# Running sums kept in device memory, and products that start on filled banks, in a hybrid attention block

## The chip, the core and the metric

The kernel runs on one core of a Trainium2 chip. The metric is the device time of one execution in microseconds; smaller is better. A core has five engines with a queue of instructions each: TensorE (PE; its weight loads are shown as PEld), VectorE (DVE), ScalarE (ACT), GpSimd (POOL) and SyncE (SP). Each runs its instructions in the order of the program and waits on semaphores where it needs another's result. Transfers are issued from SP's queue, and, where they add to what is at their destination, from GpSimd's.

## The reference, cut to what matters

The program is one decoder block on 512 tokens of width 2048, in float32. The attention half (two head groups, of 8 heads each) is not touched by the change, apart from one small step. What matters here is the second half:

```
h = h + mixed @ w_out                       # h: 512 x 2048, the residual
hn2 = rmsnorm(h, norm2_g)
h = h + (silu(hn2 @ w_gate) * (hn2 @ w_up)) @ w_down      # hidden width 5632
return rmsnorm(h, final_g)
```

## The kernel before, in words

All matrices lie transposed: 128 features on the partitions, 512 tokens along the free axis. Every weight tile is split into a high part (fp32r, ScalarE, L136) and the rest (VectorE, L139), and each product is the sum of three matmuls: high by high, high by low, low by high. The tile of a split is called a half: 128x512 of weights, four 128x128 matrices. `next_half` (L174) hands out halves in the order of the list `jobs`; before it does, `split_to` issues the splits three halves ahead (`first` is the optional preparation on VectorE and the high part on ScalarE, `second` the low part and what follows it, such as the load of a later tile). Five buffers hold the split halves, so a split waits for TensorE to be done with the half five before. `later(n, f)` puts a step f into the program when n more halves have been handed out; this is how the evacuations of a product are placed between the splits on VectorE's and ScalarE's queues.

The feed-forward part has 44 blocks of 128 hidden features (`FB`). For a block, gate and up are computed together by Strassen's scheme in Winograd's form: seven products P1 to P7 instead of eight, each of two halves, each half 4 x 3 matmuls of 128 x 128 by 128 x 256 tokens. The operands on the token side (B11, T1 and so on) are made once. The weight combinations are made block by block on VectorE in place in the raw tiles (`comb`, L778). The order in a block is P1, P7, P4, P6, P5, P2, P3 (`ORDER`). P2 is added onto P1's bank and P3 onto P5's by TensorE itself; all other sums of products are made by VectorE from the banks (`after`, L1055 to L1089), in the two tiles g and u. Then come Silu on ScalarE (L1045), u*g on VectorE (L1048), its high part h on ScalarE (L1049) and its low part on VectorE (L1053). These last steps of a block run while the next block's first products are on TensorE.

After every four blocks, in the block with f%4 == 0, 16 down products (`down`, L1091) are put between that block's products, 24 matmuls each, and VectorE adds each one's bank to the residual `hs` (L1106), which lies in SBUF as 16 tiles of 128x512. In the first round it also multiplies `hs` by `inv` (L1105), which undoes the norm's scaling. The last four blocks' down products are in `last` (L1132), which also does the final norm and the output.

Each raw weight tile (128x1024) is loaded on SP's queue into one of four buffers (`LA`), at the places named in `quad_jobs` (`nxt`). Tiles made by `placed` begin 16 or 32 elements into their buffer. The token-side operands begin at 32, the split weights of the feed-forward part at 16, except for the halves marked `even`: the first half of P1 in blocks 1 and 2 and where f%8 == 5 (L819).

Of the kernel before, what the change touches and what calls it, by code (L numbers as in the profile page):

```python
# [71 lines left out]
def block_kernel(ctx: ExitStack, tc: tile.TileContext, xt, wst, wdn, smalls, wg, w2c, bias, ident_in, out):  # L72
# [5 lines left out]
    base = ctx.enter_context(tc.tile_pool(name="base", bufs=1))  # L78
    wp = ctx.enter_context(tc.tile_pool(name="wp", bufs=1))
    ps = ctx.enter_context(tc.tile_pool(name="ps", bufs=1, space=bass.MemoryType.PSUM))  # L80

    def placed(pool, n, at, **kw):

# [315 lines left out]
    def compressed(s):  # L399
        pt = ps.tile([128, 512], F32, tag="misc", name="phidt")  # L400
        for hb in range(2):
            for i in range(2):
                pe.matmul(pt[:, 64 * hb:64 * hb + 64], hids[:, s, 128 * hb:128 * hb + 128],
                          ident[:, 64 * i:64 * i + 64], start=(i == 0), stop=(i == 1))
        h = hidt[s]
        for hb in range(2):
            c = slice(64 * hb, 64 * hb + 64)
            if s == 0:
                act.activation(h[:, hb, 0, :], pt[:, c], AF.Silu)
            else:  # L410
                for g in range(2):
                    c = slice(64 * hb + 32 * g, 64 * hb + 32 * g + 32)
                    act.activation(h[:, hb, g, :, :], pt[:, None, c].to_broadcast([128, 3, 32]), AF.Silu)
        yield
        p2 = ps.tile([128, 512], F32, tag="misc", name="pcmp")
        if s == 0:
            for hb in range(2):
                pe.matmul(p2[:, :64], w2[:, hb, :], h[:, hb, 0, :], start=(hb == 0), stop=(hb == 1))
            dve.tensor_copy(kc, p2[:, :64])
        else:  # L420
            for g in range(2):
                for hb in range(2):
                    pe.matmul(p2[:96, 128 * g:128 * g + 128], h[:, hb, g, :, :],
                              w2[:, 2 + hb, :], start=(hb == 0), stop=(hb == 1))
                v = et_h[:, 7 + 3 * g, :]
                act.activation(v[:96], p2[:96, 128 * g:128 * g + 128], AF.Copy)
                dve.tensor_tensor(v[32:64], p2[32:64, 128 * g:128 * g + 128], v[32:64].bitcast(F32), op=OP.subtract)
# [336 lines left out]
    def load_fin(n):  # L764
        while len(fin) < min(n, KB // 2):
            k = 2 * len(fin)
            fin.append(wp.tile([128, 1024], F32, tag="raw", name="fin", bufs=LA))
            sp.dma_start(fin[-1].rearrange("p (n c) -> p n c", n=2), wdn[NPH - 1, k:k + 2].rearrange("n p c -> p n c"))

    def quad_jobs(f, order):  # L770
# [17 lines left out]
        for k in range(2):  # L788
            A11, A21, A22, A12 = (lambda i=i, k=k: q(i, k) for i in range(4))

            if f == 0:
                r["P1", k] = Job(A11, load=None if k else nxt(-1), post=fetch(A11, 1, k))
                r["P5", k] = Job(A21, post=fetch(A21, 0, k))
                r["P7", k] = Job(A11)
                r["P2", k] = Job(A12)
                r["P4", k] = Job(A22, prep=comb(A12, A21))
                r["P6", k] = Job(A21)
                r["P3", k] = Job(A12)
            else:
# [62 lines left out]
    def close_attention():  # L862
# [16 lines left out]
        def close():  # L879
# [8 lines left out]
            rest["hs"] = ffn.tile([128, KB, S], F32, name="hs")  # L888
# [61 lines left out]
    def terms(nb):  # L950
# [41 lines left out]
        def s3():  # L992
            dve.scalar_tensor_tensor(t[:, HI], k[:, LO], gk, t[:, LO], op0=OP.mult, op1=OP.add)
            low("T3", n, t[:, LO])
            high("T2", n, t[:, HI])

        def s4():
            dve.scalar_tensor_tensor(t[:, LO], h[:, LO], g, t[:, HI], op0=OP.mult, op1=OP.subtract)
            low("T2", n, t[:, HI])
            high("T4", n, t[:, LO])  # L1000

        def s5():
# [16 lines left out]
             for n, t in (("P1", "proj"), ("P7", "proj"), ("P4", "sc"), ("P6", "sc"), ("P3", "t"))}  # L1019
    banks["P5"] = ps.tile([128, 512], F32, tag="o", name="P5")  # L1020
    dbanks = {}

    st = {}

    def product(f, name):
        key = {"P2": "P1", "P3": "P5" if f else "P3"}.get(name, name)
        if key == name:
            st[key] = banks[name]
        p = st[key][:, :256]
# [1 line left out]
        for k in range(2):  # L1031
            h, l = next_half()
            for s in range(4):
                mm(p, h[:, 128 * s:128 * s + 128], l[:, 128 * s:128 * s + 128], th[:, 4 * k + s, :],
                   tl[:, 4 * k + s, :], key == name and k == 0 and s == 0, k == 1 and s == 3)

    def mm(o, wh, wl, mh, ml, start, stop):
        pe.matmul(o, wh, mh, start=start, stop=False, skip_group_check=True)  # L1038
# [16 lines left out]
    def after(f, name):  # L1055
# [10 lines left out]
        g, u = st.get("g"), st.get("u")  # L1066
        if name == "P1":
            st["g"] = ft()
            st["u"] = ft() if f else None
            act.activation(st["g"][:, LO], x("P1"), AF.Copy)  # L1070
        elif name == "P6":
            sub(g[:, HI], g[:, LO], x("P6"))
            add(u[:, LO], g[:, HI], x("P7"))
            if not f:
                dve.tensor_tensor(g[:, LO], x("P1"), st["r2"][:, LO], op=OP.mult)
                add(u[:, HI], u[:, LO], x("P5"))
                sub(u[:, LO], u[:, LO], x("P4"))
                add(g[:, HI], g[:, HI], x("P5"))
        elif name == "P5":
            add(u[:, HI], u[:, LO], x("P5"))  # L1080
            sub(u[:, LO], u[:, LO], x("P4"))
        elif name == "P2":
            dve.tensor_tensor(g[:, LO], x("P1"), st["r2"][:, LO], op=OP.mult)
            if f == FB - 1:
                finish(f, g, u, LO)
        elif name == "P3":
            add(g[:, HI], g[:, HI], x("P5" if f else "P3"))
            dve.tensor_tensor(g[:, HI], g[:, HI], st["r2"][:, HI], op=OP.mult)
            finish(f, g, u, HI if f == FB - 1 else slice(0, 512))  # L1089

    def down(ph, nb):  # L1091
# [9 lines left out]
                   al[:, 12 + i, c], i == 0, i == PH - 1)  # L1101

        def add():
            if not ph:
                dve.tensor_tensor(hs[:, nb, :], hs[:, nb, :], st["inv"], op=OP.mult)  # L1105
            dve.tensor_tensor(hs[:, nb, :], hs[:, nb, :], p, op=OP.add)  # L1106

        later(1, add)

    for kind, a, b in sched:  # L1110
        if kind == "d":
# [20 lines left out]
    def last():  # L1132
        todo = deque()
        sacc = ft("sacc")
        sqt = ft("sqt")
# [4 lines left out]
        def scaled(r, nb, n, th):  # L1140
            h = hs[:, nb:nb + n, (LO, HI)[th]]
            o = h
            if th:
                if nb % 4 == 0:
                    st["o"] = wp.tile([128, 1024], F32, tag="raw", name="scaled", bufs=LA)
# [134 lines left out]
```

## Time and profile before

| | us |
|---|---|
| median of 3 runs | 2176.18 |
| lowest, highest | 2175.72, 2179.32 |
| the profiled execution | 2175.39 |
| its span, first to last instruction | 2173.6 |

| engine | busy us | share of the span |
|---|---|---|
| PE | 2159.9 | 99% |
| PEld | 2021.9 | 93% |
| DVE | 1566.0 | 72% |
| ACT | 965.9 | 44% |
| POOL | 42.7 | 2% |

The feed-forward blocks begin at 836 us and the last stage at about 2110 us. Rows of the profile have the form: line, engine, operation, tile written <- tiles read, partitions x elements and types, count | busy us, mean ns of one | idle time before them and what ended it. Rows of the timeline begin with the start and the duration in us. Matmuls overlap, so a duration of 0.28 us is not the distance from one to the next; that distance is read from the starts. Rows of a stage have its limits, its length, and then the busy time and count of PE, PEld, DVE, ACT and POOL, the granted clock, the DMA share and GB/s; where one engine was asked for, only its own.

### The profile page before, as it was taken

The page shows a single profiled execution, that of the slowest core. Times are in us where ns is not written, and L with a number is a line of the kernel's source. Part 1 is how long each engine was busy: PE and PEld are TensorE (multiplying, and loading weights), DVE is VectorE, ACT ScalarE, POOL GpSimd, SP SyncE. Part 2 cuts the span into 40 slices and gives each one's busy share as a digit, 9 for nine tenths or more (in the row PEclk, how much of TensorE's full clock was granted, in tenths as well). Part 3 has the DMA queues.
Part 4 walks back from the last instruction along what each step waited for, and adds up shares of the span by engine and source line. Part 5 has one row for each costly group of instructions (what it writes and reads, how often), then busy time and mean ns, then how long its engine had stood idle before and what let it go on. Part 6 is the DMA issues. An engine that isn't in the chain of part 4 may idle for free.

```text
span 2173.6 us, 39728 instructions
## 1 busy us (share of the span) xinstructions
PE 2159.9 (99%) x15776; PEld 2021.9 (93%) x15776; DVE 1566.0 (72%) x3046; ACT 965.9 (44%) x1862; POOL 42.7 (2%) x51
## 2 busy tenths in 40 slices
PE   9999999999999999999999999999999999999997
PEld 7888888888888889999999999999999999999997
DVE  6755565456667588979687777869596877878686
ACT  6544444344444255525343443435253434434356
POOL 0000000000000000000000000000000000000003
PEclk9999999999999999999999999999999999999999
DMA  6442222322224334333333333333333333333233
GB/s 224 150 135 80 90 77 70 102 80 81 80 78 164 98 97 101 115 116 100 108 105 117 97 109 106 108 96 108 117 98 107 108 117 92 114 107 108 81 124 107
DMA packets 81866, 232.28 MB, mean 107 GB/s; under 512 B 8848, under 2 KB 11536, under 8 KB 81680
## 3 DMA queue, kind: packets, MB, share of 16 engines
q1 hardware_dynamic: 80960, 228.17, 33.4%
q0 software_dynamic: 720, 1.57, 0.4%
q8 instruction: 124, 2.03, 0.4%
q14 instruction: 62, 0.51, 0.1%
HBM read 225.51 MB, written 4.19 MB: 106 GB/s over the span
## 4 chain that ended last, share of the span: by engine, by line
PE 98%; DVE 1%; ACT 0%; DMA 0%; issue 0%; SPq 0%; DVEq 0%; ACTq 0%
PE P L1040 15%; PE P L1038 15%; PE P L1039 15%; PE pp L167 7%; PE pp L169 7%; PE pp L168 7%; PE pd L1040 4%; PE pd L1039 4%; PE pd L1038 4%; PE pab L169 3%; PE pab L167 3%; PE pab L168 3%; PE pt L533 1%; PE po L168 1%; PE psc L169 1%; PE po L167 1%
## 5 line engine op out<-in xcount | busy, mean ns | idle before, releaser
L136 ACT ACTIVATE wh<-raw 128x512 fp32r<-128x512 f32 x888 | 548.7, 628 | 528.0 <-PE P L1039 208.7
L139 DVE TENSOR_TENSOR wl<-raw,wh 128x512 fp32r<-128x512 f32 x888 | 599.5, 687 | 43.9 <-ACT wh L136 42.5
L1040 PE MATMUL P<-ah,wl 128*128 128x256 f32 x1552 | 428.9, 276 | 0.2 <-DVE wl L139 0.2
L1038 PE MATMUL P<-ah,wh 128*128 128x256 f32 x1552 | 428.8, 276 | 0.0
L1039 PE MATMUL P<-al,wh 128*128 128x256 f32 x1552 | 428.8, 276 | 0.0
L1040 PEld LDWEIGHTS P<-ah,wl 128*128 128x128 f32 x1552 | 291.4, 188 | 0.4 <-DVE wl L139 0.4
L1039 PEld LDWEIGHTS P<-al,wh 128*128 128x128 f32 x1552 | 291.4, 188 | 0.0
L1038 PEld LDWEIGHTS P<-ah,wh 128*128 128x128 f32 x1552 | 291.4, 188 | 0.0
L167 PE MATMUL pp<-ah,wh 128*128 128x512 f32 x640 | 260.6, 407 | 0.0
L169 PE MATMUL pp<-ah,wl 128*128 128x512 f32 x640 | 251.1, 392 | 0.0
L168 PE MATMUL pp<-al,wh 128*128 128x512 f32 x640 | 250.3, 391 | 0.0
L778 DVE TENSOR_TENSOR raw<-raw 128x512 f32<-128x512 f32 x346 | 237.7, 687 | 3.4
L1040 PE MATMUL pd<-ah,wl 128*128 128x256 f32 x784 | 216.6, 276 | 0.0
L1039 PE MATMUL pd<-al,wh 128*128 128x256 f32 x784 | 216.5, 276 | 0.0
L1038 PE MATMUL pd<-ah,wh 128*128 128x256 f32 x784 | 216.5, 276 | 0.0
L136 ACT ACTIVATE wh<-rawd 128x512 fp32r<-128x512 f32 x160 | 101.1, 632 | 249.1 <-PE pd L1039 122.9
L1106 DVE TENSOR_TENSOR hs<-hs,pd 128x512 f32<-128x512 f32 x98 | 67.4, 688 | 122.0 <-PE pd L1040 121.7
L1038 PEld LDWEIGHTS pd<-ah,wh 128*128 128x128 f32 x784 | 147.2, 188 | 0.0
L1040 PEld LDWEIGHTS pd<-ah,wl 128*128 128x128 f32 x784 | 147.2, 188 | 0.0
L1039 PEld LDWEIGHTS pd<-al,wh 128*128 128x128 f32 x784 | 147.2, 188 | 0.0
L169 PEld LDWEIGHTS pp<-ah,wl 128*128 128x128 f32 x640 | 120.2, 188 | 28.1 <-DVE wl L139 0.4
L139 DVE TENSOR_TENSOR wl<-rawd,wh 128x512 fp32r<-128x512 f32 x160 | 110.1, 688 | 42.6 <-ACT wh L136 37.5
(275 smaller groups left out, 4560.0 us busy)
## 6 DMA issues: line engine op xcount, KB each, us to landing
raw<-in_wst_dram SPq DMA_DIRECT2D x310, 512.0 KB, 3.5
rawd<-in_wdn_dram SPq DMA_DIRECT2D x160, 256.0 KB, 2.6
bias<-in_bias_dram SPq DMA_DIRECT2D x16, 320.0 KB, 3.0
xc<-in_xt_dram SPq DMA_DIRECT2D x16, 256.0 KB, 3.0
hs<-in_xt_dram SPq DMA_DIRECT2D x16, 256.0 KB, 5.4
fin<-in_wdn_dram SPq DMA_DIRECT2D x8, 512.0 KB, 4.1
out_dram<-hs SPq DMA_DIRECT2D x8, 256.0 KB, 2.1
out_dram<-scaled SPq DMA_DIRECT2D x3, 512.0 KB, 2.8
```

Of the source, the lines that this page charges most:

```text
L136: act.activation(self.h, self.src(), AF.Copy)
L139: dve.tensor_tensor(self.l, self.src(), self.h.bitcast(F32), op=OP.subtract)
L167: pe.matmul(o, wh, mh, start=start, stop=False)
L168: pe.matmul(o, wh, ml, start=False, stop=False)
L169: pe.matmul(o, wl, mh, start=False, stop=stop)
L533: pe.transpose(p[:, 128 * (o + b):128 * (o + b) + 128], self.e[t][:, 128 * b:128 * b + 128], ident)
L778: return lambda: dve.tensor_tensor(o(), o(), x(), op=OP.add)
L1038: pe.matmul(o, wh, mh, start=start, stop=False, skip_group_check=True)
L1039: pe.matmul(o, wh, ml, start=False, stop=False, skip_group_check=True)
L1040: pe.matmul(o, wl, mh, start=False, stop=stop, skip_group_check=True)
L1106: dve.tensor_tensor(hs[:, nb, :], hs[:, nb, :], p, op=OP.add)
```

## The change

- The residual goes to device memory. In blocks 1 and 2, `put_away` multiplies a tile of `hs` by `inv` and stores it in `kept_sums`; the tile's SBUF is given back. A down product's bank is copied by ScalarE to one of four staging tiles, and a transfer from GpSimd's queue adds it to `kept_sums`. In blocks 41 and 42 `bring_back` loads the 16 tiles into SBUF again.
- The order in a block becomes P1, P4, P6, P5, P7, P2, P3. ScalarE copies P1's bank onto P6's, and P6's products are added on it by TensorE; the sum is copied onto P7's bank, and P7 is added there. P3 is added onto P6's bank. ScalarE also copies P4's and P5's banks to u and g. VectorE is left with five operations on banks or on their sums in place of seven. The signs of the operand T2 and of some sums change with this.
- The weight combinations are placed after P1 and before P6 accordingly; the raw tiles get a fifth buffer (`RB`), with loads still four units ahead, and the second and third tile of the next block are loaded after P7.
- Smaller edits: the gains are loaded from ScalarE's queue, the two small products of the compressed values stand before both of their copies, four of block 0's eight spreads are made by ScalarE, and block 0's product of P1 with the norm's factors moves ahead of other sums.

```diff
+    mem = ctx.enter_context(tc.tile_pool(name="mem", bufs=1, space=bass.MemoryType.DRAM))
+    kept_sums = [mem.tile([128, S], F32, name=f"sums{nb}") for nb in range(KB)]
...
+    RB = 5
...
-            t = wp.tile([128, 1024], F32, tag="raw", name="raw", bufs=LA)
+            t = wp.tile([128, 1024], F32, tag="raw", name="raw", bufs=RB)
...
-        def __init__(self, col):
+        def __init__(self, col, on_act=False):
...
-                dve.tensor_scalar(self.r[:, 128 * t:128 * t + 128], ident, col[:, t:t + 1], None, op0=OP.mult)
+                r = self.r[:, 128 * t:128 * t + 128]
+                if on_act:
+                    act.activation(r, ident, AF.Copy, scale=col[:, t:t + 1])
+                else:
+                    dve.tensor_scalar(r, ident, col[:, t:t + 1], None, op0=OP.mult)
...
-    sp.dma_start(sm, smalls)
+    act.dma_start(sm, smalls)
...
                     pe.matmul(p2[:96, 128 * g:128 * g + 128], h[:, hb, g, :, :],
                               w2[:, 2 + hb, :], start=(hb == 0), stop=(hb == 1))
+            for g in range(2):
                 v = et_h[:, 7 + 3 * g, :]
...
-                r["P1", k] = Job(A11)
-                r["P7", k] = Job(A11, prep=comb(A11, A21))
+                r["P1", k] = Job(A11, post=comb(A11, A21))
                 r["P4", k] = Job(A22, post=comb(A21, A22))
+                r["P6", k] = Job(A22, prep=comb(A22, A11))
                 r["P5", k] = Job(A21)
-                r["P6", k] = Job(A22, prep=comb(A22, A11))
+                r["P7", k] = Job(A11)
...
-                r["P5", 1].post = nxt(1)
+                r["P7", 1].post = nxt(2)
...
-    ORDER = ("P1", "P7", "P4", "P6", "P5", "P2", "P3")
+    ORDER = ("P1", "P4", "P6", "P5", "P7", "P2", "P3")
...
-            high("T2", n, t[:, HI])
+            high("T2", n, t[:, HI], -1.0)
...
+    SEEDED = ("P6", "P7")
...
-        key = {"P2": "P1", "P3": "P5" if f else "P3"}.get(name, name)
+        key = {"P2": "P1", "P3": "P6" if f else "P3"}.get(name, name)
...
-                   tl[:, 4 * k + s, :], key == name and k == 0 and s == 0, k == 1 and s == 3)
+                   tl[:, 4 * k + s, :], not (f and name in SEEDED) and key == name and k == 0 and s == 0, k == 1 and s == 3)
...
             st["g"] = ft()
-            st["u"] = ft() if f else None
-            act.activation(st["g"][:, LO], x("P1"), AF.Copy)
+            if f:
+                st["u"] = ft()
+                st["P6"] = banks["P6"]
+                act.activation(x("P6"), x("P1"), AF.Copy)
+            else:
+                act.activation(st["g"][:, LO], x("P1"), AF.Copy)
         elif name == "P6":
-            sub(g[:, HI], g[:, LO], x("P6"))
+            if f:
+                st["P7"] = banks["P7"]
+                act.activation(x("P7"), x("P6"), AF.Copy)
+                act.activation(u[:, LO], x("P4"), AF.Copy)
+                return
+            add(g[:, HI], g[:, LO], x("P6"))
+            dve.tensor_tensor(g[:, LO], x("P1"), st["r2"][:, LO], op=OP.mult)
             add(u[:, LO], g[:, HI], x("P7"))
...
-        elif name == "P5":
-            add(u[:, HI], u[:, LO], x("P5"))
-            sub(u[:, LO], u[:, LO], x("P4"))
+        elif name == "P7":
+            act.activation(g[:, HI], x("P5"), AF.Copy)
+            sub(u[:, LO], x("P7"), u[:, LO])
+            add(u[:, HI], x("P7"), g[:, HI])
...
-            add(g[:, HI], g[:, HI], x("P5" if f else "P3"))
+            if f:
+                add(g[:, HI], x("P6"), g[:, HI])
+            else:
+                add(g[:, HI], g[:, HI], x("P3"))
...
-            if not ph:
-                dve.tensor_tensor(hs[:, nb, :], hs[:, nb, :], st["inv"], op=OP.mult)
-            dve.tensor_tensor(hs[:, nb, :], hs[:, nb, :], p, op=OP.add)
+            t = st["pool"].tile([128, S], F32, tag="stg", name="stg", bufs=4)
+            act.activation(t, p, AF.Copy)
+            pool_e.dma_start(kept_sums[nb], t, accum_op=OP.add)
...
+    def put_away(nb):
+        dve.tensor_tensor(hs[:, nb, :], hs[:, nb, :], st["inv"], op=OP.mult)
+        sp.dma_start(kept_sums[nb], hs[:, nb, :])
...
+    def bring_back(nb):
...
+        sp.dma_start(st["hs"][:, nb, :], kept_sums[nb])
...
+        if name == "P5" and f in (1, 2):
+            for n in range(8):
+                later(n, lambda nb=8 * (f - 1) + n: put_away(nb))
+        if name == "P5" and f in (FB - 3, FB - 2):
+            for n in range(8):
+                later(n, lambda nb=8 * (f - FB + 3) + n: bring_back(nb))
...
-                later(1, lambda r=r: st.update(inv=Spread(r.z), r2=Spread(r.y)))
+                later(1, lambda r=r: st.update(inv=Spread(r.z, True), r2=Spread(r.y)))
...
-        elif name in ("P1", "P6", "P5", "P2", "P3"):
+        elif name in ("P1", "P6", "P7", "P2", "P3"):
```

In the kernel after the change the lines have moved down a little: the copy onto P6's bank is L1084, u*g L1060, its high part h L1061, the staging copy L1129.

More of the change, by code (lines that the diff above doesn't have):

```diff
@@ L766, in load_fin @@
             k = 2 * len(fin)
-            fin.append(wp.tile([128, 1024], F32, tag="raw", name="fin", bufs=LA))
+            fin.append(wp.tile([128, 1024], F32, tag="raw", name="fin", bufs=RB))
             sp.dma_start(fin[-1].rearrange("p (n c) -> p n c", n=2), wdn[NPH - 1, k:k + 2].rearrange("n p c -> p n c"))
@@ L887, in close @@
                                    for x, at in (("h", MH), ("l", ML)))
-            rest["hs"] = ffn.tile([128, KB, S], F32, name="hs")
+            for _ in range(2):
+                ffn.tile([128, S], F32, tag="ft", name="ft", bufs=2)
+            rest["hsp"] = ExitStack()
+            rest["hs"] = rest["hsp"].enter_context(tc.tile_pool(name="hsp", bufs=1)).tile([128, KB, S], F32, name="hs")
             for nb in range(KB):
@@ L994, in s3 @@
             low("T3", n, t[:, LO])
-            high("T2", n, t[:, HI])
+            high("T2", n, t[:, HI], -1.0)
         def s4():
             dve.scalar_tensor_tensor(t[:, LO], h[:, LO], g, t[:, HI], op0=OP.mult, op1=OP.subtract)
-            low("T2", n, t[:, HI])
+            low("T2", n, t[:, HI], -1.0)
             high("T4", n, t[:, LO])
@@ L1068, in after @@
             st["g"] = ft()
-            st["u"] = ft() if f else None
-            act.activation(st["g"][:, LO], x("P1"), AF.Copy)
-        elif name == "P6":
-            sub(g[:, HI], g[:, LO], x("P6"))
-            add(u[:, LO], g[:, HI], x("P7"))
-            if not f:
-                dve.tensor_tensor(g[:, LO], x("P1"), st["r2"][:, LO], op=OP.mult)
-                add(u[:, HI], u[:, LO], x("P5"))
-                sub(u[:, LO], u[:, LO], x("P4"))
-                add(g[:, HI], g[:, HI], x("P5"))
-        elif name == "P5":
+            if f:
[4 more added lines that the diff above has]
+                act.activation(st["g"][:, LO], x("P1"), AF.Copy)
+        elif name == "P6":
+            if f:
[5 more added lines that the diff above has]
+            dve.tensor_tensor(g[:, LO], x("P1"), st["r2"][:, LO], op=OP.mult)
+            add(u[:, LO], g[:, HI], x("P7"))
             add(u[:, HI], u[:, LO], x("P5"))
             sub(u[:, LO], u[:, LO], x("P4"))
+            add(g[:, HI], g[:, HI], x("P5"))
+        elif name == "P7":
+            act.activation(g[:, HI], x("P5"), AF.Copy)
+            sub(u[:, LO], x("P7"), u[:, LO])
+            add(u[:, HI], x("P7"), g[:, HI])
         elif name == "P2":
@@ L1103, in add @@
         def add():
-            if not ph:
-                dve.tensor_tensor(hs[:, nb, :], hs[:, nb, :], st["inv"], op=OP.mult)
-            dve.tensor_tensor(hs[:, nb, :], hs[:, nb, :], p, op=OP.add)
+            t = st["pool"].tile([128, S], F32, tag="stg", name="stg", bufs=4)
+            act.activation(t, p, AF.Copy)
+            pool_e.dma_start(kept_sums[nb], t, accum_op=OP.add)
         later(1, add)
+    def put_away(nb):
+        dve.tensor_tensor(hs[:, nb, :], hs[:, nb, :], st["inv"], op=OP.mult)
+        sp.dma_start(kept_sums[nb], hs[:, nb, :])
+        if nb == KB - 1:
+            rest["hsp"].close()
+            st["dnp"] = ExitStack()
+            st["pool"] = st["dnp"].enter_context(tc.tile_pool(name="dnp", bufs=1))
+    def bring_back(nb):
+        if nb == 0:
+            st["dnp"].close()
+            st["hs"] = ctx.enter_context(tc.tile_pool(name="fin", bufs=1)).tile([128, KB, S], F32, name="hs")
+        sp.dma_start(st["hs"][:, nb, :], kept_sums[nb])
     for kind, a, b in sched:
@@ L1144, in scaled @@
                 if nb % 4 == 0:
-                    st["o"] = wp.tile([128, 1024], F32, tag="raw", name="scaled", bufs=LA)
+                    st["o"] = wp.tile([128, 1024], F32, tag="raw", name="scaled", bufs=RB)
                 o = st["o"].rearrange("p (a b) -> p a b", b=256)[:, nb % 4:nb % 4 + n, :]
```

1 line of the change is left out of this document (added).

## The prediction

> **What bounds the kernel now.** I read the page first, then the matmul rows one by one, then VectorE's and ScalarE's rows of one block. The page names TensorE, and one stage of the feed-forward part, asked for by itself, names it without a remainder.
>
> ```profile
> span 2173.6 us, 39728 instructions
> PE 2159.9 (99%) x15776; PEld 2021.9 (93%) x15776; DVE 1566.0 (72%) x3046; ACT 965.9 (44%) x1862; POOL 42.7 (2%) x51
> ...
> 880.90:1516.20 635.30, 635.30 (x5605) 635.30 (x5605) 504.57 (x857) 271.09 (x453) 0.00 (x0) 1.00 0.35 107
> ```
>
> From 880.9 to 1516.2 us TensorE is busy 635.30 of 635.30 us. The columns after it are weight loads, VectorE (504.57), ScalarE (271.09), GpSimd, granted clock, DMA share. Busy is not yet peak, so I look at the distance between matmul starts.
>
> ```profile
> 867.78 0.28 PE L1039 MATMUL P<-al,wh 128*128 128x256 f32 x1
> 868.25 0.39 PE L1040 MATMUL P<-ah,wl 128*128 128x256 f32 x1 [0.19 <-DVE wl L139]
> 868.47 0.28 PE L1038 MATMUL P<-ah,wh 128*128 128x256 f32 x1
> ...
> 869.53 0.28 PE L1038 MATMUL P<-ah,wh 128*128 128x256 f32 x1
> ...
> 879.42 0.28 PE L1038 MATMUL P<-B11h,wh 128*128 128x256 f32 x1
> ...
> 1497.17 0.28 PE L1038 MATMUL P<-B11h,wh 128*128 128x256 f32 x1
> ...
> 1516.21 0.28 PE L1038 MATMUL P<-B11h,wh 128*128 128x256 f32 x1
> ```
>
> A block has seven products of two halves, a half has 12 matmuls. Block 23 runs from 1497.17 to 1516.21: 168 matmuls in 19.04 us, 113.3 ns each, 1.360 us a half. From 869.53 to 879.42 lie 84 matmuls of the same form in 9.89 us: 117.7 ns each, 1.413 us a half. That second pitch began after a wait (867.78 to 868.25) and lasted until block 2's first half, which takes its weights from the other offset (`even`). So TensorE has two pitches here, and one short wait cost more afterwards than while it lasted. Only blocks 1, 2 and f%8==5 have such an `even` half. The work left on TensorE does not change, so this stage cannot gain; it can only keep its pitch or lose it.
>
> **What the change can give.** Two waits of the profile are aimed at.
>
> ```profile
> PE pcmp L423 <- DVE et_h L427: 0.7, 1, 0.7
> ...
> PE P L1038 <- DVE ft L1075: 0.3, 1, 0.3
> ```
>
> The two products of L423 now stand before both copies: 0.6 off, a copy's semaphore round trip being all that is left. In block 0 the multiplication that frees P1's bank (L1075) moves from third to second place and four of the eight spreads go to ScalarE: 0.4 off with its restart. The gains' load (L280) moves from SP's queue to ScalarE's, where it stands behind the first activation; x and weights start earlier, the gains later, and the first split needs both: 0, between +0.5 and -0.5. Together -1.0 us.
>
> **The cost, part by part.** The 160 additions of down products leave VectorE, 16 multiplications stay but move to blocks 1 and 2, and 160 ScalarE copies with 160 transfers come in:
>
> ```profile
> L1106 DVE TENSOR_TENSOR hs<-hs,pd 128x512 f32<-128x512 f32 x98 | 67.4, 688 | 122.0 <-PE pd L1040 121.7
> L1105 DVE TENSOR_TENSOR hs<-hs,prb 128x512 f32<-128x512 f32 x16 | 10.9, 680 | 0.0
> ...
> L1045 ACT ACTIVATE ft<-ft 128x512 f32<-128x512 f32 x43 | 27.3, 635 | 16.1 <-DVE ft L1088 16.1
> ...
> raw<-in_wst_dram SPq DMA_DIRECT2D x310, 512.0 KB, 3.5
> ...
> out_dram<-hs SPq DMA_DIRECT2D x8, 256.0 KB, 2.1
> ...
> raw<-in_wst_dram POOLq DMA_DIRECT2D x4, 256.0 KB, 4.2
> ```
>
> VectorE waited 122 us for the products before these additions, so taking them away frees no time on the path. A copy of 128x512 costs ScalarE about 0.635 us; it has 2.72 us (24 matmuls) per down product: hidden. The adding transfers of before take 4.2 us from issue to landing, into SBUF. A staging buffer (four) is wanted again after four down products, 10.9 us, less the copy: 10.2. No row shows a transfer that adds into device memory; I bound it by 2.1 (a plain store of 256 KB, to the output) and 8.4 (twice the adding one): hidden at both ends, so I take 0. The 16 stores of put_away (SP's queue, blocks 1 and 2) and the 16 loads back (blocks 41 and 42) stand ahead of weight loads; the stores wait for one VectorE operation each, the loads for additions that ended a block before: 0, as a weight load is issued four halves or more before its use. The tightest is A21's, issued behind P7's last low part, about 4 us before P2, and wanted 2.1 us into P2: 6 us for a landing of 3.5, also 0; the fifth raw buffer is what lets the next A11 come while the old one still serves P7. The changed signs ride on operations that were there. The Trainium skill ("DMA: Bandwidth & Descriptors", Anatomy of one DMA) puts a GpSimd transfer at 2.0 us plus bytes/436e3, 2.6 us here as an estimate, and warns that the wait for completion is long above all when the target is HBM; by either figure the sum stays as it is.
>
> What is not hidden is the new way to P6. P6's first matmul now waits until ScalarE has copied P1's result onto P6's bank. That copy (L1084) stands in ScalarE's queue behind h (L1061), which waits for VectorE's u*g (L1060). TensorE reaches P6 two halves after P1's end, since P4 alone lies between. So the question is when u*g is done. Its rows in before, block 22 into 23:
>
> ```profile
> 1491.73 0.28 PE L1038 MATMUL P<-B21h,wh 128*128 128x256 f32 x1
> ...
> 1492.08 0.41 DVE L1061 TENSOR_TENSOR ft<-ft,P 128x256 f32<-128x256 f32 x1
> 1492.53 0.42 DVE L1064 TENSOR_TENSOR ft<-ft,P 128x256 f32<-128x256 f32 x1
> 1492.87 0.68 DVE L139 TENSOR_TENSOR wl<-raw,wh 128x512 fp32r<-128x512 f32 x1
> 1493.59 0.69 DVE L778 TENSOR_TENSOR raw<-raw 128x512 f32<-128x512 f32 x1
> 1494.19 0.69 DVE L139 TENSOR_TENSOR wl<-raw,wh 128x512 fp32r<-128x512 f32 x1
> ...
> 1497.37 0.42 DVE L1061 TENSOR_TENSOR ft<-ft,P 128x256 f32<-128x256 f32 x1
> ...
> 1501.30 0.69 DVE L1048 TENSOR_TENSOR ft<-ft 128x512 f32<-128x512 f32 x1
> ...
> 1497.31 0.63 ACT L136 ACTIVATE wh<-raw 128x512 fp32r<-128x512 f32 x1 [0.73 <-PE P L1039]
> 1498.29 0.64 ACT L1045 ACTIVATE ft<-ft 128x512 f32<-128x512 f32 x1 [0.35 <-DVE ft L1088]
> 1498.82 0.61 ACT L136 ACTIVATE wh<-raw 128x512 fp32r<-128x512 f32 x1
> ...
> 1502.02 0.64 ACT L1049 ACTIVATE ah<-ft 128x512 fp32r<-128x512 f32 x1 [1.09 <-DVE ft L1048]
> 1502.56 0.36 ACT L1070 ACTIVATE ft<-P 128x256 f32<-128x256 f32 x1
> ```
>
> Start-to-start on VectorE they give 0.34 after a 128x256, 0.45 if the next needs it, 0.60 after a 128x512, 0.72 if the next touches the same tile; VectorE starts 0.20 after the product it waits for ends (1497.17, 1497.37), ScalarE 0.14 (1497.31); ScalarE's next follows a 128x512 after 0.53. Already in before, with u*g at 1501.30, a copy behind h ended at 1502.92. Now zero is the start of P2 (1491.73), and the next block's P6 is wanted eight halves later, at 10.88. VectorE's order in the changed kernel from there, with those steps: P7's first subtraction 0.20; the addition needs ScalarE's new copy of P5, which runs behind a weight split (0.14 + 0.53 + 0.36): 1.07; low part 1.41, combination 2.13, low 2.73, combination 3.45, P2's product 4.05, low 4.39, combination 4.99, P6's combination 5.71, low 6.31, combination 6.91, P3's addition 7.51 (P3 ended at 5.44), product 7.97, combination 8.31, low 8.91, low 9.70 (behind Silu and its split on ScalarE, 9.03 to 9.66), u*g 10.30 to 10.99. Then h 11.02, the copy 11.56 to 11.92, TensorE about 12.0: **late by 1.1 us**, or by 0.7 where the halves take 1.413 (wanted at 11.30). In before u*g stood at 9.57. Two combinations more stand ahead of it, and the chain starts with a wait for ScalarE. Without that wait and the same-tile steps it is late by 0.1 (in the 113 pitch); with one more step of 0.6, by 1.7. I take 1.1, since every step has a row.
>
> Block 4k+1 is free of it: the down products before it leave VectorE idle, so the chain starts at P3's end, 5.64, and needs about 4.4 to the copy's end: 10.2 at worst. P7's copy has two halves, 2.72 us, and needs 1.1: free.
>
> Block 1 in before, with the start of its third product and its u*g:
>
> ```profile
> 864.95 0.28 PE L1038 MATMUL P<-T4h,wh 128*128 128x256 f32 x1
> ...
> 866.30 0.69 DVE L1048 TENSOR_TENSOR ft<-ft 128x512 f32<-128x512 f32 x1
> ```
>
> The sum, over the blocks:
> - 29 blocks from 6 to 43 and block 4 are late. In 5 of them (6, 14, 22, 30, 38: the block before was put right by its `even` half) 1.1 each, 5.5; in 25, 0.7 each, 17.5.
> - Blocks 2 and 3 also have put_away's eight multiplications before them, four inside the chain at 0.60: 1.1 + 0.7 + 2 x 2.4 = 6.6. Block 1, whose chain starts behind block 0's six evacuations, I put 3.0 later than now (u*g at 866.30 already in before; a copy would end 1.62 later, as in the walk, and P6, now third, is wanted where the third product starts, 864.95 less block 0's 0.4: 3.4 late, of which block 1 has 0.4 now).
> - The first matmul behind a wait takes 0.11 more (868.25 to 868.47): 33 times, 3.6.
> - After each wait the pitch stays at 117.7 ns until the next `even` half: block 2's last 10 halves, 3, 4, then of every eight blocks all but the `even` one and four halves, 814 halves with the down products counted double, and some 23 in the last stage: 837 x 0.053 = 44.4.
> - Gains: -1.0.
>
> 5.5 + 17.5 + 6.6 + 3.0 + 3.6 + 44.4 - 1.0 = 79.6. The profiled execution took 2175.4 us (span 2173.6 and 1.8 around it), 0.8 under the median of 2176.2: 2175.4 + 79.6 = **2255 us**.
>
> **The rivals.**
> - *It waits, but the pitch comes back by itself* (0.10). All late blocks then cost 1.1: 33.0 + 7.0 + 3.0 + 3.6 - 1.0 = 45.6, 2221 us. Against it: the nine halves from 868.25 to 879.42 did not come back.
> - *Not slower: the copy comes in time* (0.13). If u*g comes 1.1 us sooner than walked, no block waits, the pitch holds and only the gains stay: 2174 us. It is decided at the addition behind P5's copy: were VectorE not behind by the time of P3's addition (5.64 instead of 7.51), the copy would end at 10.1. Against it: the list of steps from 1.07 has 13 large operations at 0.60, 7.8 us by itself.
> - *The transfers that add don't land in time* (0.05). Above 10.2 us a landing holds ScalarE, and each microsecond over costs one per four down products, 40 in all: at 12 us 72 more, above 2300.
> - *The waits bring the clock down* (0.04). At the start the same warm-up product runs at two rates:
>
> ```profile
> 1.43:4.21 2.78, 2.78 (x15) 1.00 0.77 200
> 4.33:5.22 0.89, 0.89 (x11) 1.00 0.98 325
> ```
>
> 15 in 2.78 us against 11 in 0.89: less than half the rate for 2.8 us. If each of the 33 waits brought that back, half of 2.8 us is lost each time, 46 us instead of the pitch's 44.4, on top of all blocks at 1.1: about 2267 us. The wait at 868 did not do so. The Trainium skill ("TensorE: Matmul & The Clock Gate", A second HAM failure mode) tells of such short idles between groups bringing the clock down; by it this rival would hold, and the matmuls after 868.47 do not agree.
>
> **How the numbers follow.** The forecast has 0.68; its own range is 2234 (late by 0.5 and 0.1) to 2270 (0.4 more). The range of 8 in 10 leaves out the not-slower case: 2205, below the second case, to 2280. The bound of 0.2% is 4.4 us, about what a measurement can tell from no change. The not-slower case falls mostly inside it: faster 0.04, same 0.09, slower 0.87.
>
> **What would show it.** TensorE's waits name ScalarE's L1084 before P6 some 33 times, about 1 us each, none in blocks 5, 9, 13; halves take 1.41 us after them and 1.36 behind block 5's first; h sits behind u*g; no wait of ScalarE's staging copy (L1129) for a transfer; TensorE at 2100 us of busy time or more. Wrong if P6 starts on time in block 6, or if its matmuls return to 113 ns within a half.

## The result, and the profile after

| | before | after |
|---|---|---|
| median, us | 2175.95 | 2262.54 |
| lowest to highest, us | 2174.80 to 2179.94 | 2250.55 to 2265.61 |
| the profiled execution, us | 2175.39 | 2250.55 |
| its span, us | 2173.6 | 2248.7 |

The change makes the kernel slower: the ratio of the times is 1.038, with a 95% interval from 1.036 to 1.040. (One further execution of the changed kernel, at a granted clock of 0.65, counts in the median, but is left out of the highest time and of the ratio; the median of the other five is 2262.24.) The forecast was 2255 us in 2205 to 2280, 7.5 under the median. The profiled execution of the changed kernel is the lowest of its times, 12 us under their median; what follows about places and prices speaks of that execution.

The page of the changed kernel, first its span and busy times, then two groups (the first matmul of each three and the GpSimd transfers), the chain by engine, and four rows of transfers with their median landing:

```profile
span 2248.7 us, 40167 instructions
PE 2203.7 (98%) x15776; PEld 2058.1 (92%) x15776; DVE 1451.5 (65%) x2796; ACT 1080.5 (48%) x2155; POOL 181.4 (8%) x211
...
L1050 PE MATMUL P<-ah,wh 128*128 128x256 f32 x1552 | 437.4, 282 | 31.2 <-ACT P L1084 30.9
...
PE 86%; DVE 7%; issue 4%; ACT 3%; ACTq 0%; DVEq 0%
...
L1130 POOL DMA_DIRECT2D sums<-stg x160 | 138.6, 866 | 1150.3 <-ACT stg L1129 1042.7
...
raw<-in_wst_dram SPq DMA_DIRECT2D x310, 512.0 KB, 4.0
...
sums<-stg POOLq DMA_DIRECT2D x160, 256.0 KB, 4.5
sums<-hs SPq DMA_DIRECT2D x16, 256.0 KB, 2.1
hs<-sums SPq DMA_DIRECT2D x16, 256.0 KB, 5.4
```

VectorE has 114 us less work, ScalarE 115 more, and TensorE the same 15776 matmuls. Yet TensorE's busy time rises by 44 us, in the main because the same matmuls lie farther apart (the edges of the waits count as busy too). The rest is idle time, and the group of P6's first matmuls names its cause, the copy at L1084. Transfers: GpSimd waits for ScalarE's staging copies (1042.7 of 1150.3 us), and no wait of ScalarE's staging copy (L1129) for a transfer is among its waits.

TensorE's waits by what ended them (total, times, longest) say the same:

```profile
PE P L1050 <- ACT P L1084: 30.9, 35, 3.3
...
PE P L1050 <- DVE ft L1104: 0.8, 2, 0.4
PE P L1050 <- DVE ft L1094: 0.6, 1, 0.6
```

The wait for `pcmp` is gone. Two that the prediction did not have stand in its place: L1104 at the ends of blocks 1 and 2, and L1094, which is twice the 0.3 that L1075 had before.

Now the chain of block 22 into 23, first TensorE's rows (start, duration), then VectorE's and ScalarE's. Zero, the start of P2, is 1531.35; the prediction's walk has the same zero.

```profile
1531.35 0.28 PE L1050 MATMUL P<-B21h,wh 128*128 128x256 f32 x1
...
1536.79 0.28 PE L1050 MATMUL P<-B11h,wh 128*128 128x256 f32 x1
...
1542.12 0.28 PE L1052 MATMUL P<-T4h,wl 128*128 128x256 f32 x1
1543.43 0.38 PE L1050 MATMUL P<-ah,wh 128*128 128x256 f32 x1 [1.04 <-ACT P L1084]
1543.65 0.28 PE L1051 MATMUL P<-al,wh 128*128 128x256 f32 x1
1543.77 0.28 PE L1052 MATMUL P<-ah,wl 128*128 128x256 f32 x1
```

```profile
1531.55 0.42 DVE L1076 TENSOR_TENSOR ft<-P,ft 128x256 f32<-128x256 f32 x1
1532.42 0.42 DVE L1073 TENSOR_TENSOR ft<-P,ft 128x256 f32<-128x256 f32 x1 [0.45 <-ACT ft L1100]
...
1541.15 0.69 DVE L142 TENSOR_TENSOR wl<-raw,wh 128x512 fp32r<-128x512 f32 x1 [0.18 <-ACT wh L139]
1541.76 0.68 DVE L1060 TENSOR_TENSOR ft<-ft 128x512 f32<-128x512 f32 x1
```

```profile
1532.03 0.37 ACT L1100 ACTIVATE ft<-P 128x256 f32<-128x256 f32 x1
...
1542.48 0.63 ACT L1061 ACTIVATE ah<-ft 128x512 fp32r<-128x512 f32 x1 [0.84 <-DVE ft L1060]
1543.01 0.37 ACT L1084 ACTIVATE P<-P 128x256 f32<-128x256 f32 x1
```

Counted from zero, P7's subtraction starts at 0.20 (walked 0.20), the addition that waits for the copy of P5 at 1.07 (1.07), u*g at 10.41 (10.30), h at 11.13 (11.02), the copy ends at 12.03 (11.92), and P6 starts at 12.08 instead of 10.88: late by 1.20 (1.1). From the matmul before it, P6's first stands 1.31 us away instead of 0.11. Where the halves run at 117.7 ns the same distance is 0.88, late by 0.77 (0.7).

The last view is a surprise in block 3. Its rows have the limits, the length, TensorE's busy time and count, granted clock, DMA share and GB/s; the last row is P6's first matmul there.

```profile
908.00:911.50 3.50, 3.50 (x32) 1.00 0.40 146
911.50:914.80 3.30, 0.68 (x5) 0.91 0.52 168
914.80:920.00 5.20, 5.20 (x35) 0.73 0.43 115
...
914.20:917.50 3.30, 3.00 (x14) 0.50 0.22 52
```

```profile
914.50 0.58 PE L1050 MATMUL P<-ah,wh 128*128 128x256 f32 x1 [2.62 <-ACT P L1084]
```

In this wait of 2.62 us the granted clock falls: it is 0.50 from 914.2 to 917.5 us (0.73 over the third stretch, which also holds what follows), and P6's first twelve matmuls stand 213 ns apart, not 118. It costs about 1.4 us, once.

### The profile page after: what moved, and what is told of

Its sections match the earlier page's. It is cut to its first block, busy times and chain, and to the rows that moved or that the text cites. A ratio compares the mean times of both kernels' runs of the same rounds, so it can differ in the third digit from the quotient of the medians.

```text
span 2248.7 us, 40167 instructions
## 1 busy us (share of the span) xinstructions
PE 2203.7 (98%) x15776; PEld 2058.1 (92%) x15776; DVE 1451.5 (65%) x2796; ACT 1080.5 (48%) x2155; POOL 181.4 (8%) x211
## 4 chain that ended last, share of the span: by engine, by line
PE 86%; DVE 7%; issue 4%; ACT 3%; ACTq 0%; DVEq 0%
PE P L1050 12%; PE P L1051 12%; PE P L1052 11%; PE pp L170 7%; PE pp L172 7%; PE pp L171 7%; PE pd L1050 4%; PE pd L1052 4%; PE pd L1051 4%; PE pab L170 3%; PE pab L171 3%; PE pab L172 3%; DVE wl L142 3%; DVE raw L786 1%; ACT wh L139 1%
## 5 line engine op out<-in xcount | busy, mean ns | idle before, releaser
L142 DVE TENSOR_TENSOR wl<-raw,wh 128x512 fp32r<-128x512 f32 x888 | 602.1, 687 | 176.8 <-ACT wh L139 170.5
L1050 PE MATMUL P<-ah,wh 128*128 128x256 f32 x1552 | 437.4, 282 | 31.2 <-ACT P L1084 30.9
L142 DVE TENSOR_TENSOR wl<-rawd,wh 128x512 fp32r<-128x512 f32 x160 | 110.7, 692 | 265.9 <-ACT wh L139 259.5
L786 DVE TENSOR_TENSOR raw<-raw 128x512 f32<-128x512 f32 x346 | 238.2, 688 | 6.5
L1130 POOL DMA_DIRECT2D sums<-stg x160 | 138.6, 866 | 1150.3 <-ACT stg L1129 1042.7
```

What stands on the lines that cost most here:

```text
L142: dve.tensor_tensor(self.l, self.src(), self.h.bitcast(F32), op=OP.subtract)
L786: return lambda: dve.tensor_tensor(o(), o(), x(), op=OP.add)
L1130: pool_e.dma_start(kept_sums[nb], t, accum_op=OP.add)
```

## The experiments

The theory was: the copy in P6's way costs the time, directly by the wait and afterwards by the pitch that the wait leaves behind; transfers and filled banks cost nothing by themselves. The rivals: the transfers or their staging cost something (then undoing the products alone would not bring the time back), filling a bank costs something even in time, or the slow pitch has another cause than the waits. Line numbers in an experiment's rows are its own; they differ by a few from the changed kernel's.

**The copy goes ahead of h.** Changed kernel; ScalarE's copy onto P6's bank is issued one half earlier, and so ahead of h.

```diff
-        if name == "P1":
+        if name == "seed":
+            st["P6"] = banks["P6"]
+            act.activation(x("P6"), x("P1"), AF.Copy)
+        elif name == "P1":
...
-                st["P6"] = banks["P6"]
-                act.activation(x("P6"), x("P1"), AF.Copy)
...
+            if name == "P1":
+                later(0, lambda f=f: after(f, "seed"))
```

> The changed kernel with one move: the copy of P1's bank onto P6's is put into ScalarE's queue one half earlier, ahead of h (which waits for VectorE's u*g) instead of behind it. Theory (the wait at P6 is the copy's place behind h, and the lost pitch is a consequence of the waits): by the walk the copy then ends at 9.9 us after P2's start and P6 is wanted at 10.9, so the waits on it vanish from block 4 on; in blocks 1 to 3, where the eight multiplications stand in the chain, 1.5 to 2 us each stay, and the 117.7 ns pitch stays until block 5. About 2185 us. Rival A (the handing over of a bank from TensorE to ScalarE and back is itself too long for two halves): waits of 0.5 us or more stay in all blocks, above 2220. Rival B (the transfers or staging copies of the down products cost the time): no change, 2250 to 2265.

2184.23 us, ratio 1.0035 (1.0022 to 1.0048): moving one copy gives back 78 of 87 us. Its waits of TensorE, and the stage from 1000 to 1519 us:

```profile
PE P L1050 <- ACT P L1081: 3.0, 3, 1.3
...
PE P L1050 <- DVE ft L1105: 1.6, 2, 0.8
```

```profile
1000.00:1519.00 519.00, 519.00 (x4581) 1.00 0.54 139
```

From block 5 on TensorE has no idle time and 113.3 ns a matmul (519.00 / 4581), with all 160 adding transfers, the staging and the fifth raw buffer in place: they are hidden. What is left over the kernel before lies in blocks 1 to 4: waits before P6 (1.50, 0.95, 1.01), waits at the ends of blocks 1 and 2 (0.96 each), and the slow pitch, 2.4 in block 4 alone. Without put_away (the products alone with the copy ahead of h, below) only block 1's 1.50 is still there: it stands behind block 0's sums, and the others come from put_away, which fills VectorE's queue.

**The stores of the residual spread out too.** The same, with put_away over blocks 1 to 3, from P6 on.

```diff
-        if name == "P5" and f in (1, 2):
-            for n in range(8):
-                later(n, lambda nb=8 * (f - 1) + n: put_away(nb))
+        if name == "P6" and f in (1, 2, 3):
+            for n in range(6 if f == 1 else 5):
+                later(n, lambda nb=(0, 6, 11)[f - 1] + n: put_away(nb))
```

> As the run before, and the 16 multiplications that put the sums away are spread over blocks 1, 2 and 3 (6, 5, 5), in the stretch from P5 to P2 where VectorE has least to do, instead of 8 each in blocks 1 and 2 that reach into the next block's chain. Theory: the waits of blocks 2 and 3 vanish too, block 1's (about 2 us, behind block 0's evacuations) stays: 2177 us, level with the kernel before within 0.2%. Rival (blocks 2 and 3 wait for the stores in SP's queue, not for VectorE): as the run before, about 2185.

A miss: 2186.33 us, in two groups of three (2182 and 2191). The waits before P6 in blocks 2 and 3 are gone, but the ends of blocks 1 to 3 still wait for VectorE (0.96, 0.88, 0.20), since the multiplications now stand ahead of P2's product, and block 4 has the slow pitch again:

```profile
PE P L1050 <- DVE ft L1105: 1.5, 2, 0.8
PE P L1050 <- ACT P L1081: 1.3, 1, 1.3
```

The profiled run is of the lower group; what the upper group's 9 us are isn't seen in any trace. In neither of the two placements tried did VectorE take 16 further operations in these blocks without TensorE waiting.

**The products alone.** Changed kernel with the residual in SBUF, added to by VectorE as before.

```diff
-            t = st["pool"].tile([128, S], F32, tag="stg", name="stg", bufs=4)
-            act.activation(t, p, AF.Copy)
-            pool_e.dma_start(kept_sums[nb], t, accum_op=OP.add)
+            if not ph:
+                dve.tensor_tensor(hs[:, nb, :], hs[:, nb, :], st["inv"], op=OP.mult)
+            dve.tensor_tensor(hs[:, nb, :], hs[:, nb, :], p, op=OP.add)
...
-                later(n, lambda nb=8 * (f - 1) + n: put_away(nb))
...
-                later(n, lambda nb=8 * (f - FB + 3) + n: bring_back(nb))
```

> One half of the change alone: products on filled banks, new order and fifth raw buffer as in the changed kernel, but the sums stay in SBUF and VectorE adds the down products as before. Theory: the waits at P6 stay (0.8 us, or 1.2 in the 113 ns pitch, in three blocks of four), those of blocks 2 and 3 shrink to the common size since no multiplications stand in their chain: about 2253 us. Rival B (transfers and staging copies cost it): 2180 or less.

2253.47 us, 1.0349 (1.0333 to 1.0364), nine tenths of the loss:

```profile
PE P L1049 <- ACT P L1083: 24.7, 34, 3.3
```

The late blocks have the same distances as in the changed kernel, 0.88 and 1.31. Blocks 2 and 3 now have 1.02 and 0.88 instead of 3.05 and 2.90, which shows that put_away made them long.

**The sums alone.** Kernel before, with `kept_sums`, put_away, bring_back and the adding transfers as in the changed kernel.

```diff
+            t = st["pool"].tile([128, S], F32, tag="stg", name="stg", bufs=4)
+            act.activation(t, p, AF.Copy)
+            pool_e.dma_start(kept_sums[nb], t, accum_op=OP.add)
```

> The other half alone, on the kernel before: sums in device memory, staging copies, transfers that add, the multiplications and stores in blocks 1 and 2, the loads back; order and evacuation of products as before. Theory: no product waits for a copy, and the transfers are hidden; VectorE is 2.4 us late in blocks 2 and 3, which may cost a few tenths at a late split and with it the pitch for three blocks: 2176 to 2181 us. Rival B: above 2200.

2184.05 us, 1.0036 (1.0023 to 1.0049): 8 us slower than before, 3 more than expected at most. The added waits are all in blocks 1 to 3, for VectorE, on which put_away's multiplications stand; some 3 us of the 8 are the slow pitch that they leave until block 5:

```profile
PE P L1046 <- DVE wl L142: 2.4, 3, 1.1
...
PE P L1044 <- DVE ft L1089: 1.5, 2, 0.7
```

From block 5 on the pitch is 113.3 ns as before, without an idle time of TensorE. So device memory for the sums costs its way in, not its use.

**The products alone, with the copy ahead of h.** Both of the edits above.

> Products on filled banks with the copy onto P6's bank ahead of h, and the sums left in SBUF: the change without its late copy and without its multiplications in blocks 1 and 2. Theory: what the run with the copy ahead of h still lost beside the kernel before lies in blocks 1 to 4 (2.7 and 2.1 and 1.2 us of waits in blocks 1, 2 and 3, and 3.6 of slow pitch from there to block 5), and the multiplications cause it from block 2 on; without them 6.9 us go: 2177 us, level with the kernel before within 0.2%, block 1's wait behind block 0 being left. Rival (the filled banks cost something of their own in every block): 2184 or more.

2178.86 us beside 2179.42 for the kernel before on the same chip; ratio 1.0003 (0.9994 to 1.0012), no difference. The first row is its page's, the second the stage that the prediction read for the kernel before (there 635.30 with 5605 matmuls):

```profile
PE 2160.6 (99%) x15776; PEld 2022.9 (93%) x15776; DVE 1542.6 (71%) x2956; ACT 1001.6 (46%) x1995; POOL 42.7 (2%) x51
```

```profile
880.00:1516.00 636.00, 635.98 (x5609) 1.00 0.35 107
```

A bank that ScalarE has filled costs nothing when the filling is in time. It gains nothing either: VectorE's 23 us less are no time of TensorE's. What stays is block 1's wait before P6, 1.50 us; the lowest times, 2176.75 and 2175.49, stand 1.3 apart.

**The pitch without a wait.** Kernel before, without the `even` halves of the feed-forward blocks.

```diff
-        r["P1", 0].even = f in (1, 2) or f % 8 == 5
```

> The kernel before with one line taken out: no half of P1 takes its weights from the other offset. No wait is added and no work is changed. Theory (the pitch that a wait or a single-rate product leaves behind stays until such a half): block 0's 117.7 ns stay from there to the end, 43 blocks of 14 halves and 160 down products counted double, 922 halves at 0.053, less the nine that were slow anyway: 48 us more, about 2224 us. Rival (the pitch recovers by itself within a block or two): 2180 or less.

2225.22 us, 1.0221 (1.0207 to 1.0235). The same stage:

```profile
880.00:1516.00 636.00, 636.00 (x5402) 1.00 0.34 102
```

TensorE is busy without a gap at a clock of 1.00, yet 5402 matmuls take 636.00 us, where with `even` halves 5605 took 635.30: 117.7 ns each, in every block to the end. 49 us of loss without any wait; this is the second part of the changed kernel's loss by itself. Left alone, the pitch never came back here.

**An `even` half behind each wait.** Changed kernel; P6's second half takes the other offset in every block.

```diff
+        r["P6", 1].even = f > 0
```

> The changed kernel, and in every block P6's second half, which follows the wait, takes its weights from the other offset, as P1's first half does in blocks 1, 2 and f%8==5. Theory (that half puts the pitch right): from P5 on every block runs at 113 ns, which takes off about 28 of the 31 us of slow pitch; each such half costs 0.1, and the waits grow from 0.8 to 1.2 us as P6 is wanted sooner: about 2236 us. Rival (the pitch is drawn anew at the wait whatever the offset, and the offset does nothing): 2250 to 2265, half pitches of 117.7 ns as often as before.

2239.91 us, 1.029 (1.0275 to 1.0304):

```profile
PE P L1051 <- ACT P L1085: 40.8, 38, 3.3
...
867.50:874.20 6.70, 5.84 (x27) 0.50 0.37 98
894.80:898.00 3.20, 3.20 (x17) 0.50 0.48 148
918.70:922.00 3.30, 3.15 (x15) 0.50 0.22 52
```

The halves at 117.7 ns fall to a sum of 7 us, and nearly all blocks wait the longer 1.31 in place of 0.88, since TensorE comes to P6 sooner: the distances over pitch add up to 48.3 us instead of 37.6. Healing the pitch without taking away the wait returns 24 us (31 in the changed kernel's blocks) and makes the waits dearer by 11. The last three rows are stretches of blocks 1 to 3 with a granted clock of 0.50, 13.2 us in all against 3.3 in the changed kernel; half of the difference, some 5 us, is lost by that (an estimate). Profile against profile (2240.06 and 2250.55) 10.5 us are left.

**The copy of P5 early.** Changed kernel; ScalarE's copy of P5's bank is issued behind P5, not behind P7, so the chain starts without its wait for ScalarE.

```diff
-        elif name == "P7":
+        elif name == "P5":
             act.activation(g[:, HI], x("P5"), AF.Copy)
+        elif name == "P7":
...
-        elif name in ("P1", "P6", "P7", "P2", "P3"):
+        elif name in ("P1", "P6", "P5", "P7", "P2", "P3"):
```

> The changed kernel with ScalarE's copy of P5's bank made two halves earlier, behind P5 and not behind P7, so that VectorE's addition behind P7 no longer waits for it. Theory (the chain from P2's start to the copy at P6 is one unbroken row of VectorE's steps): the chain starts 0.4 us sooner, and every wait at P6 shrinks by about 0.4: from 1.2 to 0.8 at 113 ns, from 0.8 to 0.4 at 117.7; 32 waits, about 12 us off, near 2248, and the waits on the copy sum to 19 us instead of 31. Rival (the chain starts later, at P3's addition or at a load): the waits stay as they are.

2249.02 us, 1.0323 (1.03 to 1.0346):

```profile
PE P L1050 <- ACT P L1084: 12.2, 12, 3.3
```

The distances shrink from 1.31 to 0.77 and from 0.88 to 0.37: 0.5 us of the lateness was that one wait at the start of the chain. Their sum falls to 20.9 us, 16.7 less, but the time only by some 13: a wait of 0.3 us leaves the slow pitch behind as well as one of 0.8 (37 us of it in this run).

**The small edits alone.** Kernel before with the gains' load, the order of the two small products, the four spreads on ScalarE and the moved multiplication in block 0.

> The kernel before with the small edits alone: the gains' load on ScalarE's queue, the two small products ahead of both copies, four spreads on ScalarE and P1's product earlier in block 0. Predicted: 0.6 off at the small products, 0.4 off at block 1's first product, 0 at the start: 1.0 us off, 2175 us, inside what can be measured; in the profile the wait of 0.7 at the small products is gone and the one of 0.3 before block 1 is gone or smaller.

2174.81 us, 0.9987 (0.9978 to 0.9996): 0.13% faster, the only version that is faster than the kernel before by more than the noise; all 11 of its times (2174.14 to 2175.21) lie under the lowest of 15 of that kernel (2175.46). The first product of block 1 no longer waits for VectorE, nor the two small products of the compressed values; a wait of 0.6 in block 1 takes some of it back:

```profile
PE P L1045 <- DVE wl L139: 0.6, 1, 0.6
```

## Why the prediction was right

Term by term, for the profiled execution, from the matmul starts:

| term | predicted, us | measured, us |
|---|---|---|
| the 30 late blocks | 5.5 + 17.5 | 26.8 (8 at 1.20, 21 at 0.77, block 38 at 1.06) |
| blocks 2 and 3 | 6.6 | 5.7 |
| block 1, beyond its wait of before | 3.0 | 3.1 |
| first matmul after a wait | 3.6 | 4.4 (40 times 0.11) |
| blocks 4k+1 | 0 | 1.7 |
| slow pitch | 44.4 | 30.4 (31.0 in the blocks, 1.1 in the last stage, less 1.7 of before) |
| half the clock in block 3 | in a rival | 1.4 |
| ends of blocks 1 and 2 | 0 | 1.2 |
| gains | -1.0 | -0.9 and +0.3 |
| sum | 79.6 | 74.1 of 75.2 |

That the sum comes so near is in part luck: the slow pitch was put 14.0 us too high, and the other terms together 8.5 too low.

- *TensorE is the floor, and the stage cannot gain.* Right: with the copy in time the products alone are level with the kernel before, though VectorE has 23 us less to do.
- *Late by 1.1, or 0.7 at the slow pitch.* Right to 0.1, with every step of the walk within 0.11. The copy behind h is shown as the cause: ahead of h, no block from 4 on waits.
- *Blocks 1 to 3.* Right in size: 9.6 predicted, 8.8 measured. What the prediction missed is that put_away also makes P2's product late and so the next block's P1 (0.58 at the ends of blocks 1 and 2).
- *Block 4k+1 is free of it.* Only in part. Three of the ten (9, 33, 41) start P6 in time, those that TensorE reaches at the slow pitch; the other seven wait 0.14 to 0.33. The copy ended at 11.0 to 11.2, counted from P3's end at 5.44, not at 10.2 at worst. From VectorE's addition of P3 to the copy's end it took 4.5 us, as walked (4.4); but in block 13 that addition starts 1.0 later than P3's end allows, because a low part and a combination of the next weights stand ahead of it (block 12 into 13):

```profile
1247.67 0.68 DVE L142 TENSOR_TENSOR wl<-raw,wh 128x512 fp32r<-128x512 f32 x1
1248.27 0.68 DVE L786 TENSOR_TENSOR raw<-raw 128x512 f32<-128x512 f32 x1
1248.87 0.42 DVE L1073 TENSOR_TENSOR ft<-P,ft 128x256 f32<-128x256 f32 x1
```

- *Slow pitch, 837 halves.* Mis-sized, and this is the step that failed: "after each wait the pitch stays at 117.7 ns until the next `even` half". It stays where no wait comes (blocks 2 to 43 of the kernel without `even` halves), but a wait does more than leave a slow pitch: it draws the pitch anew. Of the 40 waits before P6, 11 went from 113 to 118 and 6 stayed at 113; of those that met 118, 7 left 113, and 16 left 118 (block 3, after its stretch at half the clock, among them). Block 6, which the prediction named for its sign of being wrong, is one of the seven: it waits, but behind the wait its matmuls run at 113.3 ns (21 in the 2.38 us from 1022.77 to 1025.15), and so that sign came true:

```profile
1021.44 0.28 PE L1052 MATMUL P<-T4h,wl 128*128 128x256 f32 x1
1022.32 0.38 PE L1050 MATMUL P<-ah,wh 128*128 128x256 f32 x1 [0.60 <-ACT P L1084]
...
1022.77 0.28 PE L1050 MATMUL P<-ah,wh 128*128 128x256 f32 x1
...
1025.15 0.28 PE L1050 MATMUL P<-T1h,wh 128*128 128x256 f32 x1
```

The slow time is 30.4 us in place of 44.4. The median execution is 12 us longer than the profiled one; 226 more slow halves at 0.053 would be that, and the run of the products alone did have more of them (43 us). Lost clock is the other candidate: the executions of 2262.24 and 2265.61 us have a mean granted clock of 0.994, where the profiled one has 0.997, and 0.003 of 2262 is some 7 us. It can't be all, since the one of 2258.74 us is 8 us longer at 0.997. Neither share is shown.
- *The rival "pitch comes back by itself"* does not hold: a wait left 113 ns in 13 cases of 40, and between waits the pitch never went back but at `even` halves. (The nine halves that the prediction set against it are eight: 868.25 to 879.42 at 1.413.) *The rival "transfers don't land"*: 4.5 us against the 10.2 allowed, inside the bounds of 2.1 and 8.4. *The rival "the copy comes in time"* is what moving it made true.
- *The rival "the waits bring the clock down"* was put at every wait; in the profiled execution it took place in one of 40. The Trainium skill ("TensorE: Matmul & The Clock Gate", A second HAM failure mode) speaks of short idles between groups that do so; here the 37 waits up to 1.31 us left the granted clock at 1.00, and only one of the three distances of 2.9 to 3.6 us did it.
- *Gains.* The feed-forward part begins at 835.5 instead of 836.4 us, 0.9 earlier, the `pcmp` wait and 0.2 more. Block 0's 0.4 did not come: one more combination and low part (L786, L142) stand ahead of the multiplication on VectorE, so P1's bank is free 0.3 later, not earlier. With the small edits alone, which leave those away, that wait is gone.
- *Transfers, staging, loads: 0.* Right in use. ScalarE waits more for down weights (82.3 us in 48 waits, 40.4 in 28 before), but none reached TensorE.

What stays open: what decides which of the two pitches a wait leaves, what makes the changed kernel's other executions longer than the profiled one, and the upper group of the run with the stores spread out.

## What to carry to other kernels

When an operation becomes a *precondition* of the bottleneck's next work, walk the queue of the engine that does it: an operation that was harmless behind a long chain (here behind h) must then stand ahead of it, and one moved line was worth 78 of 87 us. Count also what a stall leaves behind: here the slower pitch afterwards cost 30 us beside 38 of waits. Work taken off an engine that is not the bound was worth nothing by itself, and 16 operations and stores put into two full blocks cost 8 us though 160 later ones were saved.

## What the runs showed of the hardware

- The same matmuls run at 113.3 or 117.7 ns, both at a granted clock of 1.00. The slow pitch lasted from block 2 to block 43, the last, in the kernel without `even` halves; it goes back to 113 at a half whose weights lie at the other offset, and a wait before a product may change it either way (in the run with `even` halves behind each wait, 35 of 43 waits went from 113 to 118 and 5 stayed).
- Of ten distances of 2.9 to 3.6 us between two matmuls (three in the changed kernel, three each with the `even` halves and with the early copy of P5, one with the products alone), six were followed by matmuls 207 to 214 ns apart; the 30-odd of 0.3 to 1.4 us in each of these runs never were. The granted clock in those six stretches was 0.50, for 3.2 us or more, in one for 6.7. The length of the distance did not decide it: the 3.60 us in block 1 did it in two of these four runs and not in the other two.
- A 256 KB transfer that adds into device memory landed in 4.5 us (4.2 into SBUF before), and its issue kept GpSimd 0.87 us.
